# A two-layer decoder trunk on one core: the opening's order, two chunks in a spare buffer, and biases loaded already repeated

## The chip, the core and the metric

The kernel runs on one core of a Trainium2 chip. The metric is the device time of one execution in microseconds (us). A core has a matrix engine (TensorE, PE in the rows; its weight loads are listed apart as PEld), a vector engine (VectorE, DVE), a scalar engine (ScalarE, ACT), GpSimd (POOL) and SyncE (SP), which here only issues transfers. Each engine works through its own instructions in order and waits at an instruction whose operands are not there yet. Transfers run on 16 DMA engines beside them.

## What is computed

```
c_act = silu(c)
for i in range(2):
    sh1, sc1, g1, sh2, sc2, g2 = split(c_act @ ada_w[i] + ada_b[i], 6)
    h = rms_norm(x, norm_mix_g[i]) * (1 + sc1) + sh1
    y = chunk_sgu_mixer(h) if i == 0 else forgetting_attention(h)
    x = x + g1 * y
    h = rms_norm(x, norm_ffn_g[i]) * (1 + sc2) + sh2
    x = x + g2 * ((silu(h @ w_gate[i]) * (h @ w_up[i])) @ w_down[i])
out = rms_norm(x, final_g)

def chunk_sgu_mixer(h):                 # x and h: 256 positions x 2048
    u, v = split(gelu(h @ w_in + b_in)) # w_in 2048 x 4096
    v = layer_norm(v, ln_g, ln_b)
    sv = tril(w_s) @ v + b_s            # in chunks of 128 positions, 16 groups
    return (u * sv) @ w_out
```

Everything is float32. ada_w alone is 2 x 2048 x 12288; a program that reads every weight once moves about 600 MB.

## The kernel before, in words

**Chunks.** Weights come as chunks of 1 MB, a tile of 128 partitions x 4 x 512 named raw, from a pool of five places. SyncE issues their transfers in program order and waits before each until its place is free. An ada chunk (a quarter of one set of four column blocks of a modulation vector) is loaded in ada_chunk (line 153). A weight chunk of w_in is loaded in wchunk (line 303). In the opening the ada chunks are called a0, a1, ... here and the chunks of w_in w0, w1, ..., both in the order of their issue: a0 to a7, w0, a8, w1, a9, a10, w2, a11, w3, a12, a13, w4 and so on.

**What frees a place.** The first 32 ada chunks are multiplied on TensorE (line 169, four matmuls each, into one PSUM bank named misc for a set of four chunks); later ones are multiplied on VectorE (lines 178 and 183). After a set, ada_sum copies the bank by ScalarE into kept (line 195), sums its partitions with four small matmuls (line 198), and VectorE adds the sums to the modulation table mod (line 202). A weight chunk is split: ScalarE casts each half to a rounded high part hi (line 290), and VectorE or GpSimd subtracts to get the low part lo (line 294). Its place is free when both halves are split; there are four buffers each for hi and lo, that is two chunks.

**The first projection.** prepare and modulate make four row blocks of h (tile hA): VectorE scales (line 449), ScalarE adds the shift and writes the high part (line 453), VectorE the low part (line 458). The first such call needs a0 to a3 (shift) and a4 to a7 (scale). v_group multiplies a chunk by hA with three matmuls per row block (lines 351 to 353) into two PSUM banks of the pool mm, which has six; VectorE then adds the result to the tile v (line 547). u_group does the same with lines 335 to 338 and four banks. The loop runs over four quarters of the 2048 rows; in each come four v groups and four u groups, one weight chunk per group, and about one to one and a half ada chunks between two groups. w0 to w3 belong to the first four v groups, v0 to v3, and w4 to w7 to the u groups.

**The opening.** x is loaded into two tiles xt, squared and summed on ScalarE (line 503), and transposed by TensorE into xT (line 519), each bank copied out by ScalarE (line 524). Small tables are transposed on TensorE (lines 122, 126, 138). The bias of v is one row of 2048, loaded to one partition (line 530), repeated to all 128 partitions by four matmuls with ones (line 533), and copied to both halves of v by eight ScalarE copies (line 537). Later the spatial bias b_s (line 575) is repeated in the same way, four times a matmul (line 593) and a ScalarE copy (line 594).

A scheduler orders the instructions of each engine, except inside tc.manual_schedule, where the written order holds; tc.issue_after places an instruction behind another one.

Of the kernel before, what the change touches and what calls it, by code (L numbers as in the profile page):

```python
# [8 lines left out]
F32 = mybir.dt.float32  # L9
# [24 lines left out]
def trunk_kernel(  # L34
# [38 lines left out]
    def misc():  # L73
        return psx.tile([P, 512], F32, tag="misc", name="misc")
# [46 lines left out]
    pt = misc()  # L121
    nc.tensor.transpose(out=pt[:, :96], in_=rows_a, identity=ident[:96, :96])
    nc.vector.tensor_copy(out=cols, in_=pt[:, :96])
    ln_cols = const.tile([P, 32], F32, name="ln_cols")
    pt = misc()
    nc.tensor.transpose(out=pt[:, :32], in_=rows_c, identity=ident[:32, :32])
    nc.vector.tensor_copy(out=ln_cols, in_=pt[:, :32])
# [8 lines left out]
    for i in range(2):  # L136
        pt = misc()
        nc.tensor.transpose(out=pt[:, :96], in_=rows_b[i], identity=ident[:96, :96])
        nc.vector.tensor_copy(out=mod[i], in_=pt[:, :96])
# [9 lines left out]

    def ada_chunk(layer, v, b0, q):  # L150

        raw = rawp.tile([P, 4, 512], F32, tag="raw", name="raw")
# [344 lines left out]
    for q in range(4):  # L497
        ada_next()
    x_ss = const.tile([P, NB], F32, name="x_ss")
    x_rs = const.tile([P, NB], F32, name="x_rs")  # L500
    junk = new_half("junk", F32).rearrange("p a b -> p (a b)")
    for t in range(NB):
        nc.scalar.activation(
            out=junk[:, D * t : D * t + D], in_=xt[t], func=AF.Square,
            accum_out=x_ss[:, t : t + 1],
        )
    rsqrt(x_rs, x_ss, D, NB)
    pt = misc()
    for t in range(NB):
        nc.tensor.matmul(  # L510
            pt[:, P * t : P * t + P], lhsT=x_rs[:, t : t + 1].to_broadcast([P, P]), rhs=ident,
            start=True, stop=True,
        )
    nc.vector.tensor_copy(out=rstd, in_=pt[:, :T])
    for k in range(0, KT, 2):
        pt = misc()
        for b in range(2):
            for t in range(NB):
                nc.tensor.transpose(
                    out=pt[:, T * b + P * t : T * b + P * t + P],  # L520
                    in_=xt[t][:, P * (k + b) : P * (k + b) + P],
                    identity=ident,
                )
        nc.scalar.copy(out=xT[:, k : k + 2, :], in_=pt.rearrange("p (b t) -> p b t", b=2))
# [3 lines left out]
    u = [mgp.tile([P, 8, T], F32, tag="mg", name="u") for _ in range(2)]  # L528
    v = [mgp.tile([P, D], F32, tag="mg", name="v") for _ in range(NB)]
    nc.scalar.dma_start(out=v[1][0:1, :], in_=a_b_in[0:1, D : 2 * D])  # L530
    for a in range(0, D, 512):
        pt = misc()
        nc.tensor.matmul(
            pt, lhsT=ones[0:1, :], rhs=v[1][0:1, a : a + 512], start=True, stop=True
        )
        for t in range(NB):
            nc.scalar.copy(out=v[t][:, a : a + 512], in_=pt)
# [5 lines left out]
    def v_group(cg, k0, nk):  # L543
        ps = proj(mm_b, NB, win_v, D + 512 * cg, hA, k0, k0 + nk, uv_rate(k0, 1.2))
        for t in range(NB):
# [19 lines left out]
    prep(0)  # L565
    for k0, nk in ((0, 4), (4, 4), (8, 4), (12, 4)):
        if k0 == 4:
            pre = new_half("pre", F32).rearrange("p a b -> p (a b)").rearrange(
                "p (a d) -> p a d", a=2
            )  # L570
            nc.sync.dma_start(
                out=pre[:, 0, :].rearrange("t (g s) -> t g s", s=P),
                in_=a_w_s[0].rearrange("g t s -> t g s"),
            )
            nc.sync.dma_start(
                out=pre[0:1, 1, :], in_=a_b_s[0:1].rearrange("o g t -> o (g t)")
            )
# [477 lines left out]
```

## Time and profile before

| what | value |
|---|---|
| runs | 2375.45, 2370.2 and 2375.41 us, median 2375.41 us |
| the profiled execution's own time | 2370.1 us |
| its span, first to last instruction | 2368.4 us |
| TensorE busy | 2293.4 us, 97% of the span |
| VectorE, ScalarE, GpSimd busy | 69%, 47%, 26% |
| mean granted TensorE clock | 0.988 of full speed |
| first matmul of a projection | 47.74 us after the span's start |

The span is what the trace covers; the execution's own time is 1.7 us longer. Busy shares are means over the whole program, and say little of the opening, where the engines fill up one after the other.

### The profile page before, as it was taken

What the parts mean: (1) busy time and instruction counts of PE and PEld (TensorE: products, weight loads), DVE (VectorE), ACT (ScalarE), POOL (GpSimd) and SP (SyncE); (2) the same over time, 40 slices, a digit from 0 to 9 for tenths busy, and PEclk for the clock granted to TensorE, in tenths of its full rate; (3) what the DMA queues carried; (4) which work ended last, traced back from release to release, by engine and by line L of the source; (5) the groups of instructions that cost most, each with busy time, mean ns of one, the idle gap of its engine ahead of it and who ended that gap; (6) DMA issues with size and microseconds to landing.
All of it is one profiled execution on the core that took longest, in us unless ns stands there. A gap on an engine that the chain in (4) does not pass through costs nothing.

```text
span 2368.4 us, 37510 instructions
## 1 busy us (share of the span) xinstructions
PE 2293.4 (97%) x14837; PEld 2035.8 (86%) x14837; DVE 1632.0 (69%) x2382; ACT 1118.5 (47%) x1851; POOL 622.3 (26%) x379
## 2 busy tenths in 40 slices
PE   6999799999999999999999999999999999999998
PEld 3778678999988888888877888899999988888887
DVE  2356986789997777777797776677776844444564
ACT  4433644643554445544454554446444533444443
POOL 1323344444561112122211111220112411212221
PEclk8999899999999999999999999999999999999999
DMA  8878878998878788788787776689765555555552
GB/s 334 304 254 306 293 252 321 338 327 313 314 272 298 269 283 284 270 284 272 274 285 256 249 243 241 217 295 338 257 224 179 195 179 196 178 196 185 189 178 89
DMA packets 305043, 605.69 MB, mean 256 GB/s; under 512 B 11586, under 2 KB 11714, under 8 KB 304610
## 3 DMA queue, kind: packets, MB, share of 16 engines
q1 hardware_dynamic: 304578, 603.13, 73.0%
q8 instruction: 116, 1.90, 0.3%
q14 instruction: 59, 0.48, 0.1%
q0 software_dynamic: 288, 0.16, 0.0%
q10 hardware_dynamic: 2, 0.01, 0.0%
HBM read 601.15 MB, written 2.11 MB: 255 GB/s over the span
## 4 chain that ended last, share of the span: by engine, by line
PE 84%; DVE 9%; DMA 3%; ACT 2%; issue 1%; POOL 0%; SPq 0%; ACTq 0%; DVEq 0%
PE mm L333 31%; PE mm L338 25%; PE mm L336 9%; PE mm L335 9%; PE mm L351 2%; PE mm L352 2%; DVE misc L183 2%; PE mm L353 2%; DVE lo L294 2%; DMA raw<-in_a_w_in_dram 2%; PE misc L169 1%; ACT hi L290 1%; DVE gu L735 1%; DMA raw<-in_a_w_out_dram 1%; DVE m L440 1%
## 5 line engine op out<-in xcount | busy, mean ns | idle before, releaser
L290 ACT CAST hi<-raw 128x1024 fp32r<-128x1024 f32 x752 | 780.2, 1050 | 884.3 <-PE mm L333 493.6
L294 DVE TENSOR_TENSOR lo<-raw,hi 128x1024 fp32r<-128x1024 f32 x566 | 725.3, 1285 | 448.6 <-ACT hi L290 445.1
L338 PE MATMUL mm<-hA,lo 128*128 128x256 f32 x3584 | 983.1, 283 | 0.6 <-DVE lo L294 0.5
L294 POOL TENSOR_TENSOR lo<-raw,hi 128x1024 fp32r<-128x1024 f32 x186 | 471.2, 2534 | 1379.6 <-ACT hi L290 1305.6
L338 PEld LDWEIGHTS mm<-hA,lo 128*128 128x128 f32 x3584 | 681.2, 191 | 11.6 <-issue 1.1
L333 PE MATMUL mm<-hA,hi 128*128 128x512 f32 x1792 | 624.4, 398 | 8.4 <-DVE hA L458 4.5
L335 PE MATMUL mm<-hA,hi 128*128 128x256 f32 x1792 | 502.9, 285 | 7.3 <-DVE gu L735 5.6
L336 PE MATMUL mm<-hA,hi 128*128 128x256 f32 x1792 | 505.7, 284 | 0.5 <-DVE hA L458 0.5
L333 PE MATMUL mm<-m,hi 128*128 128x512 f32 x1248 | 432.7, 396 | 0.0
L333 PEld LDWEIGHTS mm<-hA,hi 128*128 128x128 f32 x1792 | 333.0, 189 | 80.2 <-DVE qk L941 4.6
L338 PE MATMUL mm<-m,lo 128*128 128x256 f32 x1408 | 383.1, 281 | 0.1
L335 PEld LDWEIGHTS mm<-hA,hi 128*128 128x128 f32 x1792 | 341.7, 192 | 16.8 <-DVE gu L735 7.6
L183 DVE SCALAR_TENSOR_TENSOR misc<-raw,cact,misc 128x512 f32<-128x512 f32 x465 | 348.2, 749 | 6.6 <-DMA raw<-in_ada_w_dram 1.0
L336 PEld LDWEIGHTS mm<-hA,hi 128*128 128x128 f32 x1792 | 344.9, 192 | 3.4 <-issue 2.4
L333 PEld LDWEIGHTS mm<-m,hi 128*128 128x128 f32 x1248 | 231.4, 188 | 49.7
L338 PEld LDWEIGHTS mm<-m,lo 128*128 128x128 f32 x1408 | 265.4, 189 | 5.6 <-DVE lo L294 0.3
L735 DVE TENSOR_TENSOR gu<-mm,gu 128x256 f32<-128x256 f32 x288 | 112.7, 415 | 52.4 <-PE mm L338 52.3
L481 DVE SCALAR_TENSOR_TENSOR xT<-mm,mod,xT 128x256 f32<-128x256 f32 x176 | 75.5, 477 | 54.1 <-PE mm L338 54.1
L351 PE MATMUL mm<-hi,hA 128*128 128x512 f32 x256 | 100.9, 401 | 3.1 <-ACT hA L453 3.1
L352 PE MATMUL mm<-lo,hA 128*128 128x512 f32 x256 | 101.6, 398 | 0.0
L353 PE MATMUL mm<-hi,hA 128*128 128x512 f32 x256 | 101.5, 398 | 0.0
L440 DVE TENSOR_TENSOR m<-mf,m 128x256 fp32r<-128x256 f32 x88 | 64.4, 743 | 14.2 <-ACT m L439 13.8
(211 smaller groups left out, 2090.8 us busy)
## 6 DMA issues: line engine op xcount, KB each, us to landing
raw<-in_ada_w_dram SPq DMA_DIRECT2D x192, 1024.0 KB, 6.0
raw<-in_ffn_w_gate_dram SPq DMA_DIRECT2D x88, 1024.0 KB, 5.4
raw<-in_ffn_w_up_dram SPq DMA_DIRECT2D x88, 1024.0 KB, 5.1
raw<-in_ffn_w_down_dram SPq DMA_DIRECT2D x88, 1024.0 KB, 5.0
raw<-in_b_w_in_dram SPq DMA_DIRECT2D x48, 1024.0 KB, 6.0
raw<-in_a_w_in_dram SPq DMA_DIRECT2D x32, 1024.0 KB, 6.9
raw<-in_a_w_out_dram SPq DMA_DIRECT2D x16, 1024.0 KB, 6.9
raw<-in_b_w_out_dram SPq DMA_DIRECT2D x16, 1024.0 KB, 5.7
```

Of the source, the lines that this page charges most:

```text
L183: nc.vector.scalar_tensor_tensor(out=acc, in0=raw[:, k, :], scalar=cact[:, kt : kt + 1], in1=acc, op0=ALU.mult, op1=ALU.add,)
L290: nc.scalar.copy(out=out_hi, in_=src)
L294: ins = eng.tensor_sub(out=out_lo, in0=src, in1=out_hi.bitcast(F32))
L333: nc.tensor.matmul(ps[j], lhsT=hi[:, js], rhs=x, start=start, stop=False)
L335: nc.tensor.matmul(o, lhsT=hi[:, js], rhs=x[:, 0:T], start=start, stop=False)
L336: nc.tensor.matmul(o, lhsT=hi[:, js], rhs=x[:, T:], start=False, stop=False)
L338: nc.tensor.matmul(o, lhsT=lo[:, js], rhs=x[:, 0:T], start=False, stop=(kt == last))
L351: nc.tensor.matmul(ps[t], lhsT=xh, rhs=hi[:, k, :], start=(kt == first), stop=False)
L352: nc.tensor.matmul(ps[t], lhsT=xh, rhs=lo[:, k, :], start=False, stop=False)
L353: nc.tensor.matmul(ps[t], lhsT=xl, rhs=hi[:, k, :], start=False, stop=(kt == last))
L440: nc.vector.tensor_sub(out=dst[:, T:], in0=src, in1=dst[:, 0:T].bitcast(F32))
L735: nc.vector.tensor_add(out=dst, in0=ps[j][:, 0:T], in1=dst)
```

## The change

The opening's TensorE work is written out inside tc.manual_schedule: x is transposed first, in three pieces, with the first ada chunks between them, and the tables follow. xT is copied out of PSUM by VectorE in place of ScalarE, from the banks mm. The first two ada chunks go to a spare tile of hpool (early, in the list places), and raw's five places serve from the third chunk on. The squares of x are written to the tile that later is u.

The bias of v and b_s are loaded by transfers that read the one row once for each of the 128 partitions (partition_broadcast), 1 MB each, on ScalarE's queue, behind the instruction made (the fourth high part of hA). w_s (1 MB) is loaded there too; it was on SyncE's queue. The eight matmuls and the ScalarE copies that repeated the biases are gone. Only v[0] gets the bias; the first v groups add it from there for both halves. The subtractions of the first four half chunks are put on VectorE (hold).

```
+    def table(dst, src):
+        n = src.shape[0]
+        pt = banks(1)[0]
+        nc.tensor.transpose(out=pt[:, :n], in_=src, identity=ident[:n, :n])
+        nc.vector.tensor_copy(out=dst, in_=pt[:, :n])
...
-        raw = rawp.tile([P, 4, 512], F32, tag="raw", name="raw")
+        raw = places.pop(0) if places else rawp.tile([P, 4, 512], F32, tag="raw", name="raw")
...
-    for q in range(4):
-        ada_next()
...
-    junk = new_half("junk", F32).rearrange("p a b -> p (a b)")
+    early = new_half("early", F32)
+    places += [early[:, 0:4, :], early[:, 4:8, :]]
+    u = [mgp.tile([P, 8, T], F32, tag="mg", name="u")]
+    junk = u[0].rearrange("p a b -> p (a b)")
...
-        nc.scalar.copy(out=xT[:, k : k + 2, :], in_=pt.rearrange("p (b t) -> p b t", b=2))
+            nc.vector.tensor_copy(
+                out=xT[:, k : k + 2, :], in_=pt.rearrange("p (b t) -> p b t", b=2)
+            )
...
+    with tc.manual_schedule(engines={nc.tensor.engine}):
+        x_columns(0, 8)
+        ada_next()
+        x_columns(8, 12)
+        ada_next()
+        x_columns(12, 16)
+        table(cols, rows_a)
+        table(ln_cols, rows_c)
+        ada_next()
+        x_scale()
+        for i in range(2):
+            table(mod[i], rows_b[i])
+        for q in range(5):
+            ada_next()
...
-    nc.scalar.dma_start(out=v[1][0:1, :], in_=a_b_in[0:1, D : 2 * D])
-    for a in range(0, D, 512):
-        pt = misc()
-        nc.tensor.matmul(
-            pt, lhsT=ones[0:1, :], rhs=v[1][0:1, a : a + 512], start=True, stop=True
-        )
-        for t in range(NB):
-            nc.scalar.copy(out=v[t][:, a : a + 512], in_=pt)
...
-        for t in range(NB):
-            dst = v[t][:, 512 * cg : 512 * cg + 512]
-            nc.vector.tensor_add(out=dst, in0=ps[t], in1=dst)
+        for t in reversed(range(NB)):
+            s = slice(512 * cg, 512 * cg + 512)
+            dst = v[t][:, s]
+
+            nc.vector.tensor_add(out=dst, in0=ps[t], in1=v[t if k0 else 0][:, s])
...
-    prep(0)
+    made, _ = prep(0)
+    pre = new_half("pre", F32).rearrange("p a b -> p (a b)").rearrange("p (a d) -> p a d", a=2)
+    with tc.issue_after(made.ins):
+        nc.scalar.dma_start(
+            out=v[0], in_=a_b_in[0:1, D : 2 * D].rearrange("o n -> (o n)").partition_broadcast(P)
+        )
+        nc.scalar.dma_start(
+            out=pre[:, 1, :],
+            in_=a_b_s[0:1].rearrange("o g t -> (o g t)").partition_broadcast(P),
+        )
+        nc.scalar.dma_start(
+            out=pre[:, 0, :].rearrange("t (g s) -> t g s", s=P),
+            in_=a_w_s[0].rearrange("g t s -> t g s"),
+        )
+    hold[:] = [((), nc.vector)] * 4
...
-                pt = misc()
-                nc.tensor.matmul(pt, lhsT=ones[0:1, :], rhs=pre[0:1, 1, gs], start=True, stop=True)
-                nc.scalar.copy(out=pre[:, 1, gs], in_=pt)
```

TensorE, from its second instruction to the first matmul of v0, before (L519 are x's transposes, L169 ada chunks of four matmuls each, L533 the bias of v):

```order
L122 MATMUL misc<-ident,rows 128x96
L126 MATMUL misc<-ident,rows 128x32
L138 MATMUL misc<-ident,rows 128x96 x2
L169 MATMUL misc<-raw,cact_142 32x512 x16
L198 MATMUL misc<-ones,kept 128x1 x4
L510 MATMUL misc<-ident,x_rs 128x128 x2
L519 MATMUL misc<-ident,xt 128x128 x32
L533 MATMUL misc<-v,ones 128x512 x4
L169 MATMUL misc<-raw,cact_142 32x512 x16
L198 MATMUL misc<-ones,kept 128x1 x4
L169 MATMUL misc<-raw,cact_142 32x512 x4
L351 MATMUL mm<-hi,hA 128x512
```

The same place of the changed kernel, from the second piece of x on (its lines are one or more higher: L515 for L519, L170 for L169, L199 for L198):

```order
L170 MATMUL misc<-early,cact_131 32x512 x4
L515 MATMUL mm<-ident,xt 128x128 x8
L136 MATMUL mm<-ident,rows 128x96
L136 MATMUL mm<-ident,rows 128x32
L170 MATMUL misc<-raw,cact_131 32x512 x4
L527 MATMUL mm<-ident,x_rs 128x128 x2
L136 MATMUL mm<-ident,rows 128x96 x2
L170 MATMUL misc<-raw,cact_131 32x512 x4
L199 MATMUL misc<-ones,kept 128x1 x4
L170 MATMUL misc<-raw,cact_131 32x512 x16
L199 MATMUL misc<-ones,kept 128x1 x4
L170 MATMUL misc<-raw,cact_131 32x512 x4
```

The bias matmuls are gone, the transposes of x stand ahead of or between the first chunks, and nothing but one short sum stands between the fourth and the fifth ada chunk.

ScalarE in the same stretch, before (L290 are the casts of weight chunks, L195 the copies of ada sums, L537 those of the bias):

```order
L195 COPY kept<-misc 128x512
L524 COPY xT<-misc 128x512 x8
L537 COPY v<-misc 128x512 x2
L290 CAST hi<-raw 128x1024
L537 COPY v<-misc 128x512 x2
L290 CAST hi<-raw 128x1024
L537 COPY v<-misc 128x512 x4
L195 COPY kept<-misc 128x512
L290 CAST hi<-raw 128x1024 x2
L453 ACTIVATE hA<-xr,mod_130 128x256 x4
```

And in the changed kernel:

```order
L196 COPY kept<-misc 128x512
L291 CAST hi<-raw 128x1024 x2
L196 COPY kept<-misc 128x512
L454 ACTIVATE hA<-xr,mod_125 128x256 x2
L291 CAST hi<-raw 128x1024 x2
L454 ACTIVATE hA<-xr,mod_125 128x256 x2
L585 DMA v<-in_a_b_in_dram 128x2048
L588 DMA pre<-in_a_b_s_dram 128x2048
L592 DMA pre<-in_a_w_s_dram 128x16x128
L291 CAST hi<-raw 128x1024 x2
```

The sixteen copies for xT and the bias have left ScalarE; the second copy of an ada sum still stands behind the two casts of w0, and three transfers are issued behind the fourth high part of hA.

## Rows read from the trace of the kernel before

**Rows 1.** The page: the span, and TensorE's busy time over it.

```profile
span 2368.4 us, 37510 instructions
PE 2293.4 (97%) x14837; PEld 2035.8 (86%) x14837; DVE 1632.0 (69%) x2382; ACT 1118.5 (47%) x1851; POOL 622.3 (26%) x379
```

**Rows 2.** Chain of waits, 20 to 60 us: start, duration, what ended last.

```profile
20.83 11.43 DMA raw<-in_a_w_in_dram
...
36.42 1.91 PE misc L169 x8
...
38.34 6.92 DMA raw<-in_a_w_in_dram
...
45.28 1.99 ACT hi L290 x2
...
47.74 0.79 PE mm L351
```

**Rows 3.** Stretches: busy time (and count) of engines, granted clock, DMA share, GB/s.

```profile
10.00:20.00 10.00, 6.35 (x31) 1.80 (x35) 1.34 (x8) 2.90 (x4) 0.00 (x0) 1.00 1.05 408
20.00:30.00 10.00, 8.96 (x56) 5.39 (x48) 0.59 (x2) 5.93 (x11) 0.00 (x0) 1.00 1.05 409
30.05:40.29 10.24, 8.13 (x25) 1.98 (x28) 1.23 (x1) 5.38 (x9) 2.35 (x1) 0.50 0.30 100
40.29:47.10 6.81, 3.68 (x32) 1.37 (x24) 1.95 (x5) 2.40 (x3) 0.00 (x0) 1.00 1.05 404
47.10:53.94 6.84, 6.20 (x18) 3.22 (x19) 4.93 (x7) 2.00 (x5) 2.46 (x1) 0.50 1.05 409
53.94:60.00 6.06, 6.06 (x28) 5.03 (x27) 1.55 (x2) 1.41 (x2) 0.00 (x0) 1.00 1.05 401
117.00:150.00 33.00, 33.00 (x155) 24.06 (x155) 14.26 (x27) 12.80 (x16) 11.04 (x5) 1.00 0.52 185
```

**Rows 4.** Timeline, 0 to 60 us: start, duration, engine, line, and idle time before.

```profile
9.32 1.91 ACT L503 ACTIVATE junk<-xt 128x2048 f32<-128x2048 f32 x1 [1.03 <-DMA xt<-in_x_dram]
...
22.91 5.33 PE L519 MATMUL misc<-ident,xt 128*128 128x128 f32 x32
...
42.00 0.59 ACT L195 COPY kept<-misc 128x512 f32<-128x512 f32 x1 [4.47 <-PE misc L169]
...
42.63 1.05 PE L198 MATMUL misc<-ones,kept 128*128 128x1 f32 x8 [0.71 <-ACT kept L195]
...
43.62 1.06 PE L169 MATMUL misc<-raw,cact 128*32 128x512 f32 x8
...
44.12 0.88 DVE L449 SCALAR_TENSOR_TENSOR xr<-xT,acol,rstd 128x256 f32<-128x256 f32 x2
...
51.45 1.94 PE L169 MATMUL misc<-raw,cact 128*32 128x512 f32 x8
```

**Rows 5.** Timeline, 58 to 71 us, VectorE and GpSimd.

```profile
59.06 1.22 DVE L294 TENSOR_TENSOR lo<-raw,hi 128x1024 fp32r<-128x1024 f32 x1
...
60.77 2.40 POOL L294 TENSOR_TENSOR lo<-raw,hi 128x1024 fp32r<-128x1024 f32 x1 [10.96 <-ACT hi L290]
...
62.98 0.69 DVE L547 TENSOR_TENSOR v<-mm,v 128x512 f32<-128x512 f32 x1 [0.67 <-PE mm L353]
...
63.13 2.00 POOL L579 TENSOR_SCALAR_AFFINE_SELECT pre<-pre 128x2048 f32<-128x2048 f32 x1
...
70.83 0.69 DVE L547 TENSOR_TENSOR v<-mm,v 128x512 f32<-128x512 f32 x1 [0.67 <-PE mm L353]
```

**Rows 6.** Chain of waits, 112 to 160 us: the first of four such rows.

```profile
121.65 1.05 PE misc L593 x2
```

**Rows 7.** TensorE's waits, 222 to 312 us: waiter, releaser, total, times, longest.

```profile
PE misc L214 <- ACT kept L209: 9.7, 1, 9.7
PE mm L641 <- ACT v L628: 4.2, 1, 4.2
```

**Rows 8.** Tile vf: landing of four 0.5 MB transfers, repeated to 128 partitions.

```profile
DMA to landing us min/median/max: 6.3/7.0/7.7
```

More of the change, by code (lines that the diff above doesn't have):

```diff
@@ L120, in trunk_kernel @@
     cols = const.tile([P, 96], F32, name="cols")
-    pt = misc()
-    nc.tensor.transpose(out=pt[:, :96], in_=rows_a, identity=ident[:96, :96])
-    nc.vector.tensor_copy(out=cols, in_=pt[:, :96])
+    cols = const.tile([P, 96], F32, name="cols")
     ln_cols = const.tile([P, 32], F32, name="ln_cols")
-    pt = misc()
-    nc.tensor.transpose(out=pt[:, :32], in_=rows_c, identity=ident[:32, :32])
-    nc.vector.tensor_copy(out=ln_cols, in_=pt[:, :32])
     lng_col, lnb_col = ln_cols[:, 0:16], ln_cols[:, 16:32]
@@ L135, in trunk_kernel @@
     acol = [[const.tile([P, KT], F32, name=f"acol{i}_{j}") for j in range(2)] for i in range(2)]
[L136 to L139, printed above, removed]
+    def table(dst, src):
[3 more added lines that the diff above has]
+        nc.vector.tensor_copy(out=dst, in_=pt[:, :n])
     ada_v = [ada_w[i].rearrange("(kt p) (v n) -> p kt v n", p=P, n=D) for i in range(2)]
@@ L148, in trunk_kernel @@
     lo_last, paced = [], []
+    places = []
     def ada_chunk(layer, v, b0, q):
-        raw = rawp.tile([P, 4, 512], F32, tag="raw", name="raw")
+        raw = places.pop(0) if places else rawp.tile([P, 4, 512], F32, tag="raw", name="raw")
         nc.sync.dma_start(
@@ L494, in new_h @@
         return lambda kt: halves[kt // 8][:, kt % 8, :]
-    for q in range(4):
-        ada_next()
     x_ss = const.tile([P, NB], F32, name="x_ss")
     x_rs = const.tile([P, NB], F32, name="x_rs")
-    junk = new_half("junk", F32).rearrange("p a b -> p (a b)")
+    early = new_half("early", F32)
+    places += [early[:, 0:4, :], early[:, 4:8, :]]
+    u = [mgp.tile([P, 8, T], F32, tag="mg", name="u")]
+    junk = u[0].rearrange("p a b -> p (a b)")
     for t in range(NB):
         nc.scalar.activation(
-            out=junk[:, D * t : D * t + D], in_=xt[t], func=AF.Square,
-            accum_out=x_ss[:, t : t + 1],
+            out=junk, in_=xt[t], func=AF.Square, accum_out=x_ss[:, t : t + 1]
@@ L506, in trunk_kernel, with x_columns @@
         )
     rsqrt(x_rs, x_ss, D, NB)
-    pt = misc()
-    for t in range(NB):
-        nc.tensor.matmul(
-            pt[:, P * t : P * t + P], lhsT=x_rs[:, t : t + 1].to_broadcast([P, P]), rhs=ident,
-            start=True, stop=True,
-        )
[L514 to L517, printed above, removed]
-            for t in range(NB):
[L519 to L523, printed above, removed]
-        nc.scalar.copy(out=xT[:, k : k + 2, :], in_=pt.rearrange("p (b t) -> p b t", b=2))
+    def x_columns(k0, k1):
+        for k in range(k0, k1, 2):
+            pt = banks(1)[0]
+            for b in range(2):
+                for t in range(NB):
+                    nc.tensor.transpose(
+                        out=pt[:, T * b + P * t : T * b + P * t + P],
+                        in_=xt[t][:, P * (k + b) : P * (k + b) + P],
+                        identity=ident,
+                    )
+            nc.vector.tensor_copy(
+                out=xT[:, k : k + 2, :], in_=pt.rearrange("p (b t) -> p b t", b=2)
+            )
@@ new lines, in x_scale @@
+    def x_scale():
+        pt = banks(1)[0]
+        for t in range(NB):
+            nc.tensor.matmul(
+                pt[:, P * t : P * t + P], lhsT=x_rs[:, t : t + 1].to_broadcast([P, P]),
+                rhs=ident, start=True, stop=True,
+            )
+        nc.vector.tensor_copy(out=rstd, in_=pt[:, :T])
+    with tc.manual_schedule(engines={nc.tensor.engine}):
[12 more added lines that the diff above has]
+            ada_next()
@@ L526, in trunk_kernel @@
     win_v = a_w_in[0].rearrange("(kt p) n -> p kt n", p=P)
     hA = new_h("hA")
-    u = [mgp.tile([P, 8, T], F32, tag="mg", name="u") for _ in range(2)]
+    u.append(mgp.tile([P, 8, T], F32, tag="mg", name="u"))
     v = [mgp.tile([P, D], F32, tag="mg", name="v") for _ in range(NB)]
-    nc.scalar.dma_start(out=v[1][0:1, :], in_=a_b_in[0:1, D : 2 * D])
-    for a in range(0, D, 512):
-        pt = misc()
-        nc.tensor.matmul(
-            pt, lhsT=ones[0:1, :], rhs=v[1][0:1, a : a + 512], start=True, stop=True
-        )
-        for t in range(NB):
-            nc.scalar.copy(out=v[t][:, a : a + 512], in_=pt)
@@ L544, in v_group @@
         ps = proj(mm_b, NB, win_v, D + 512 * cg, hA, k0, k0 + nk, uv_rate(k0, 1.2))
-        for t in range(NB):
-            dst = v[t][:, 512 * cg : 512 * cg + 512]
-            nc.vector.tensor_add(out=dst, in0=ps[t], in1=dst)
+        for t in reversed(range(NB)):
+            s = slice(512 * cg, 512 * cg + 512)
+            dst = v[t][:, s]
+            nc.vector.tensor_add(out=dst, in0=ps[t], in1=v[t if k0 else 0][:, s])
             if k0 + nk == KT:
@@ L564, in trunk_kernel @@
     prep = prepare(0, 0, hA)
-    prep(0)
+    made, _ = prep(0)
[7 more added lines that the diff above has]
+            in_=a_b_s[0:1].rearrange("o g t -> (o g t)").partition_broadcast(P),
+        )
+        nc.scalar.dma_start(
+            out=pre[:, 0, :].rearrange("t (g s) -> t g s", s=P),
+            in_=a_w_s[0].rearrange("g t s -> t g s"),
+        )
+    hold[:] = [((), nc.vector)] * 4
     for k0, nk in ((0, 4), (4, 4), (8, 4), (12, 4)):
         if k0 == 4:
[L568 to L577, printed above, removed]
             wst = pre[:, 0, :].rearrange("t (g s) -> t g s", s=P)
```

1 line of the change is left out of this document (removed).

## The prediction

> **What bounds the kernel now.** The page first [rows 1]: TensorE is busy for 2293 of 2368 us, so work taken off TensorE, or time in which it waits, is what can be won. The opening is the largest wait. I read it in the chain of waits between 20 and 60 us [rows 2]: w0 is issued at 20.83 and has landed at 32.26; nothing about it is late. The next link is TensorE at 36.42, which multiplies a4 only then; that frees a place, w1 is issued at 38.34 and lands at 45.26, and two casts, the first high part and 0.5 us later the first projection matmul, at 47.74. The stretches say the same from the transfers' side [rows 3]: the DMA engines are full (share 1.05) from 10 to 30 us and from 40 on, and at 0.30 from 30.05 to 40.29. That is a hole of 0.7 x 10.24 = 7 us. It opens because a4 to a7 lie in their places while TensorE works through what stands ahead of them: x's transposes (5.33 us from 22.91 on [rows 4]), and the bias matmuls L533, whose banks wait for ScalarE copies that stand behind the casts of w0.
>
> From the first matmul on it is TensorE: 6.06 of 6.06 us from 53.94 on, 33.00 of 33.00 from 117 to 150, with the DMA share down to 0.52 there [rows 3]. So an earlier first matmul should move everything behind it, as long as the transfers follow.
>
> **The change, part by part.**
>
> *Where the first matmul moves.* A chunk of 1024 KB takes 1.049 MB / 408 GB/s = 2.57 us of full transfers [rows 3]. Up to w0 the same eleven MB move in the same order through engines that were full already, so w0 lands at 32.3 as before. Counting back from it, a3 landed at 19.4, a4 at 22.0 and a7 at 29.7. In the new order only chunks stand between a3 and a7 on TensorE, and four such matmuls take 1.06 us at the full clock and 1.94 at half [rows 4], both under 2.57, so each is done before the next lands. The transposes lie between the landing of x (9.3 us [rows 4]) and a3: 5.3 us of transposes and four chunks of 1.06 in 10 us. Their copies on VectorE have no row; the nearest is an addition from PSUM of the same shape, 0.69 us [rows 5], so 8 x 0.69 = 5.5 us on an engine with 1.34 busy in that stretch [rows 3]. If that cover failed, they would delay a3, which has 10 us before a7 in hand. I take nothing.
>
> With a4 to a7 freed as they land, a8, w1, a9 and a10 are issued in time and follow w0 without the hole, at 34.8, 37.4, 40.0 and 42.5 (w1 at 45.3 before).
>
> The bound is then w0 itself: on ScalarE the second copy of an ada sum stands behind its two casts. 32.3 + 1.99 (two casts [rows 2]) = 34.25. From here the old offsets hold [rows 4]: the sums follow 0.63 after the copy's start (42.00 to 42.63), the scaling 1.49 later (to 44.12), which makes 36.4; 0.47 for it (half of 0.88, rounded up) and 0.5 for the high part make 37.4. The matmuls of a8, landed at 34.8, stand behind the sums and end between 37.0 and 37.9, by the clock. I take 37.6 for the first matmul: **10.1 us earlier** than 47.74.
>
> *The spatial bias.* Its matmuls L593 go. Each of the four pairs costs 1.05 us on the chain [rows 6], in a stretch where TensorE is full [rows 3]: **4.2 us**. The bias matmuls of v lay before the first matmul and are in the 10.1 already.
>
> *Two more MB of transfers.* The two biases come as 1 MB each where 8 KB came before; w_s moves from one queue to the other. All three are issued behind the fourth high part, about 41 us, into engines that were full there [rows 3]. They add 2 x 2.57 = 5.1 us of transfers before, with w_s, 7.7 us share the engines with w2, a11, w3. What waits is v2. It needs w2 landed, cast and half subtracted: 1.0 + 1.22 [rows 2, 5] = 2.2 us. TensorE wants it when v1 is done, in the old kernel at 62.98 [rows 5], that is 15.2 us after the first matmul, so at 52.8; v3 7.85 us later (70.83 - 62.98), at 60.7. Undisturbed, w2 lands at 45.1 and is ready at 47.3: nothing is lost. If all 7.7 us go first, w2 lands at 52.8 and is ready at 55.0: 2.2 us lost. Then w3, two chunks on, lands at 58.0 and is ready at 60.2, in time. Between 0 and 2.2 I take 0, since nothing in the rows shows one queue shutting out another; 2.2 is kept for the range.
>
> The Trainium skill, page "DMA: Bandwidth & Descriptors", section "Issuing engines are not separate DMA queues", says that transfers started by different engines run on the same 16 DMA engines and interleave. By that rule ScalarE's queue buys no bandwidth, and w2 would pass at about half speed from 41 to 42 us on: it would land near 48 and be ready at 50, also in time. No row here shows two such queues at once.
>
> *Additions that wait for the bias.* v0's and v1's results stay in PSUM until v[0] has landed. Transfers that repeat a row took 6.3 to 7.7 us for 0.5 MB [rows 8], so 1 MB takes 6.3 (the size free) to 15.4 (in proportion): landed between 48 and 57. v0 and v1 hold four of six banks, v2 the other two, so the first to be refused a bank is v3, at 60.7. Nothing lost.
>
> *GpSimd.* w_s must be landed and masked (2.00 us) before GpSimd's part of w3 (2.40) [rows 5]. Landed by 57 at the latest, as the last of the three: both done by 61.4, or by 62.4 if that part waits for the second cast of w3. v3 starts with VectorE's half and asks for GpSimd's 2.7 us later, at 63.4. Nothing lost.
>
> *The clock.* It is at half (1.2 GHz) from 47.10 to 53.94, around the first matmuls, after a stretch with TensorE at 3.68 of 6.81 us [rows 3]. The new opening has TensorE at some 40% of the time between 20 and 37, and I expect about the same stretch at half behind 37.6. Bounds: none, 6.84 / 2 = 3.4 us won; as long as the one of 10.24, 1.7 lost. I take 0.
>
> *Further on.* At 264 us TensorE waits 9.7 and 4.2 us [rows 7]. The scheduler puts that copy kept ahead of casts now, but the second wait ends on the normalised v whatever the first does. VectorE's order there differs by one or two operations of 0.7 us in both directions. 0, with 2 us to either side.
>
> *Sum.* The profiled execution took 2370.1 us (span 2368.4 and 1.7 around it): 2370.1 - 10.1 - 4.2 = 2355.8. The runs stand at two levels, 2370.2 and 2375.4; the profile belongs to the lower, the median to the upper. A new median can fall to either, so I put it between: 2355.8 + 2.6 = **2358.4**.
>
> **Rivals.**
>
> *Less is passed on* (18%). The start moves, but part is lost on the way: the clock stays at half, w2 is late by its 2.2 us, or VectorE, which also bounds the stage behind 264, costs its 2. For it: all three bounds lie there. Against it: each has cover. All three: 2358.4 + 1.7 + 2.2 + 2.0 = 2364.
>
> *The transfers become the bound* (14%). TensorE's earlier start needs w2 to w7 earlier, with 5.1 us more to move. For it: from 53 to 61 us the margin that I found is 0.5 us for w3 when the loads go first. If ScalarE's three loads run as slowly as in [rows 8], 3 MB take up to 46 us, and SyncE's chunks get about half of the engines for that time. A group eats 2.5 chunks, 6.4 us of full transfers, in 7.85 us of TensorE; at half speed 12.8. 46 us at that pace are 3.6 groups with 5 us lost at each, 18 in place of 14.3 won: no change, 2358.4 + 18 = 2376. At half of that duration it is 9 us, 2367. Against it: the share is 0.52 later on.
>
> *Slower: the bias lands too late* (6%). 128 reads of one 8 KB row could be far slower than rows read once. v3 then waits for banks until v[0] is there. It decides at 60.7 + 14.3 = 75 us: a landing behind that makes the kernel slower. At a quarter of the pace of [rows 8], 62 us, v[0] lands at 103, TensorE stands from 60.7, and the time is 2358 + 43 = 2401. Against it: 7.0 us for half a MB, while other chunks were in flight.
>
> **How the numbers follow.** The forecast has the remaining 62%; its own range is 2350.4 (2355.8 less 3.4 for the clock and 2 further on) to 2364 (upper level, with one of the bounds). I give 2350 to 2369, which leaves out the upper half of the transfers' case, the slower one and little below. About 0.3%, 7 us, is what a measurement of this kernel can tell from no change. The forecast and the first rival are faster by more: 80%. The transfers' case centres on no change: 14%. Slower: 6%.
>
> **What would show it.** The first matmul of v0 at 37 to 38 us, with w0 landed at 32.3 and w1 at 37 to 38; a DMA share near 1 from 10 to 55 us without a hole; TensorE full from there on, v1's last addition near 53 and v3 not waiting; the rest of the trace 14 us earlier at the same place. The sum is wrong if TensorE waits between 50 and 75 us for casts of w2 to w4, if the additions of v0 wait for a transfer, or if the wait behind 250 us has grown.

## The result, and the profile after

The changed kernel took 2359.62 us (median of 5 runs, 2355.96 to 2362.97), the kernel before beside it 2373.43 (5 runs): a ratio of 0.9947, 95% interval 0.9936 to 0.9958. It is faster by more than the 0.3% that a measurement here can tell, and 1.2 us above the forecast. The profiled execution took 2359.62 us as well, 10.5 less than that of before.

The page of the changed kernel, to be read against [rows 1]:

```profile
span 2357.9 us, 37458 instructions
PE 2284.9 (97%) x14821; PEld 2036.9 (86%) x14821; DVE 1641.9 (70%) x2392; ACT 1107.0 (47%) x1832; POOL 618.9 (26%) x377
```

TensorE is busy for 8.5 us less, and idle for 2.0 less. The chain of waits from 20 to 72 us (start, duration, what ended last), against [rows 2]:

```profile
20.58 13.08 DMA raw<-in_a_w_in_dram
33.68 1.99 ACT hi L291 x2
35.67 0.49 ACT kept L196
36.20 1.86 PE misc L199 x8
38.07 1.86 PE misc L170 x8
39.93 0.73 PE mm L352
...
62.09 0.80 PE misc L199 x8
...
62.91 0.04 DVE mod L203
...
62.99 0.68 DVE v L564
63.67 2.00 DVE lo L295
...
65.71 0.80 PE mm L353
```

w1 is no longer a link. The start is w0 (landed at 33.66), its casts, the copy kept that stands behind them, the sums and a8. A second chain is new, at v3: the matmul of 65.71 waits for w3's first low part, which on VectorE stands behind the small addition L203 (which waits for TensorE's sums) and an addition of v2.

The stretches (busy time and count of TensorE, its weight loads, VectorE, ScalarE, GpSimd; granted clock, DMA share, GB/s), against [rows 3]:

```profile
20.00:23.60 3.60, 2.56 (x24) 1.13 (x16) 0.16 (x1) 0.59 (x1) 0.00 (x0) 1.00 1.05 410
23.60:30.00 6.40, 3.32 (x16) 0.41 (x16) 0.00 (x0) 0.00 (x0) 0.00 (x0) 0.50 1.05 405
30.00:40.00 10.00, 6.28 (x29) 2.32 (x25) 4.00 (x8) 3.46 (x6) 0.00 (x0) 0.50 1.05 409
40.00:44.10 4.10, 4.10 (x10) 3.24 (x11) 4.10 (x8) 2.62 (x5) 0.00 (x0) 0.50 1.05 409
44.10:50.00 5.90, 5.90 (x30) 3.97 (x30) 0.20 (x1) 0.00 (x0) 0.00 (x0) 1.00 1.03 424
...
64.50:71.40 6.90, 5.69 (x16) 4.00 (x20) 1.15 (x1) 1.99 (x2) 2.44 (x2) 0.51 0.89 337
```

The hole in the transfers is gone (1.05 where 0.30 stood). The clock is at half (1.2 GHz) from 23.6 to 44.1 us, and again from 64.5 to 71.4, behind v3's wait. The timeline of the same stretch, against [rows 4, 5]:

```profile
39.86 0.80 PE L352 MATMUL mm<-hi,hA 128*128 128x512 f32 x1
...
65.71 0.80 PE L353 MATMUL mm<-lo,hA 128*128 128x512 f32 x1 [2.25 <-DVE lo L295]
...
59.66 0.59 ACT L196 COPY kept<-misc 128x512 f32<-128x512 f32 x1 [6.80 <-PE misc L170]
60.14 2.00 ACT L291 CAST hi<-raw 128x1024 fp32r<-128x1024 f32 x2
...
62.22 2.35 POOL L295 TENSOR_TENSOR lo<-raw,hi 128x1024 fp32r<-128x1024 f32 x1 [3.21 <-ACT hi L291]
...
62.99 0.68 DVE L564 TENSOR_TENSOR v<-mm,v 128x512 f32<-128x512 f32 x1
63.59 2.07 DVE L295 TENSOR_TENSOR lo<-raw,hi 128x1024 fp32r<-128x1024 f32 x1
...
76.58 0.68 DVE L564 TENSOR_TENSOR v<-mm,v 128x512 f32<-128x512 f32 x1
...
97.01 0.88 DVE L450 SCALAR_TENSOR_TENSOR xr<-xT,acol,rstd 128x256 f32<-128x256 f32 x2
```

The first projection matmul comes 7.88 us earlier (39.86 for 47.74), v2's last addition 7.84 (62.99 for 70.83), v3's only 2.45 (76.58 for 79.03 in the trace of before). The POOL row is GpSimd's subtraction of w3's second half. VectorE's, which starts beside it at 63.59, takes 2.07 us where the same operation took 1.22 in [rows 5]: 0.85 us of the 2.25 come with that. The last row, the scaling of the second four columns, is a mark for the experiments: it stood at 101.65 before, so 4.64 us are in hand at 100 us.

### The profile page after: what moved, and what is told of

Same layout as the page of the kernel before. It is cut to its first block, busy times and chain, and to the rows that moved or that the text cites. A ratio compares the mean times of both kernels' runs of the same rounds, so it can differ in the third digit from the quotient of the medians.

```text
span 2357.9 us, 37458 instructions
## 1 busy us (share of the span) xinstructions
PE 2284.9 (97%) x14821; PEld 2036.9 (86%) x14821; DVE 1641.9 (70%) x2392; ACT 1107.0 (47%) x1832; POOL 618.9 (26%) x377
## 4 chain that ended last, share of the span: by engine, by line
PE 84%; DVE 9%; DMA 3%; issue 1%; ACT 1%; POOL 0%; SPq 0%; ACTq 0%; DVEq 0%; POOLq 0%
PE mm L334 32%; PE mm L339 25%; PE mm L336 9%; PE mm L337 9%; PE mm L352 2%; PE mm L353 2%; DVE misc L184 2%; PE mm L354 2%; DVE lo L295 2%; DMA raw<-in_ada_w_dram 1%; PE misc L170 1%; DMA raw<-in_a_w_in_dram 1%; DMA raw<-in_a_w_out_dram 1%; ACT hi L291 1%; DVE gu L753 1%
## 5 line engine op out<-in xcount | busy, mean ns | idle before, releaser
L441 DVE TENSOR_TENSOR m<-mf,m 128x256 fp32r<-128x256 f32 x88 | 64.5, 744 | 14.2 <-ACT m L440 13.6
```

## The experiments

Theory R (order): the order by hand closes the hole. Its rival B: the bias matmuls L533 made the hole, and it closes without them whatever the order. For v3: theory O (order on ScalarE and VectorE) against Q (the loads on ScalarE's queue). Ratios are to the runs of before on the same chip; their intervals are 0.1 to 0.2% (2 to 4 us) to either side, so small effects are read from the traces.

### What closed the hole: order_only, loads_only, v_only

order_only keeps the new TensorE order and the two places, with the old biases:

```diff
+    nc.scalar.dma_start(out=v[1][0:1, :], in_=a_b_in[0:1, D : 2 * D])
+    for a in range(0, D, 512):
+        pt = misc()
...
+            nc.scalar.copy(out=v[t][:, a : a + 512], in_=pt)
-    with tc.issue_after(made.ins):
-        nc.scalar.dma_start(
...
+                nc.tensor.matmul(pt, lhsT=ones[0:1, :], rhs=pre[0:1, 1, gs], start=True, stop=True)
+                nc.scalar.copy(out=pre[:, 1, gs], in_=pt)
```

> The changed kernel with its TensorE order and its two spare places, but with the biases as before: a row of 8 KB each, multiplied by ones on TensorE (8 matmuls for v, now behind the sums, 4 for the spatial bias) and copied by ScalarE; w_s on SyncE's queue as before. Theory R (order): the order by hand closes the hole in the transfers from 30 to 40 us; w0 and w1 land as in the changed kernel, the first matmul comes some 2 to 3 us after its 39.86 (bias matmuls of 2.07 a pair stand ahead of it), L593 costs its 4.2 us again, and v3's wait (2.25 and the half clock behind it) is smaller, since nothing shares the engines from 44 to 56: 2359.6 + 4.2 + 2.5 - 3 = 2363, still 7 us or more below before. Rival B (bias matmuls): what the change wins comes from taking the 12 bias matmuls and their 12 copies away; then this kernel is within 4 us of before.

loads_only is the kernel before with the reverse edit: both biases by repeated loads, no bias matmuls, the old order and five places.

> The kernel before with only the loads changed: both biases repeated over the partitions by transfers on ScalarE's queue, no bias matmuls and copies; TensorE's order left to the scheduler, five places. Theory R (order): the 5.33 us of x's transposes still stand between a3 and a4 at 22.9 us, so the places of a4 to a7 come free later, part of the hole stays, and the first matmul is 3 to 5 us later than the 39.86 of the changed kernel: 2363. Rival B (bias matmuls): without L533 TensorE multiplies a4 at 28.2 in place of 36.4, w1 is issued near 29.5, ahead of the end of a8's transfer, so that there is no hole at all; w0 lands at 32.3, the first matmul comes at 38 to 40, and the time is that of the changed kernel, 2358 to 2361.

v_only is the kernel before with the load of v's bias alone:

```diff
-    nc.scalar.dma_start(out=v[1][0:1, :], in_=a_b_in[0:1, D : 2 * D])
-    for a in range(0, D, 512):
...
+    with tc.issue_after(made.ins):
+        nc.scalar.dma_start(
+            out=v[0], in_=a_b_in[0:1, D : 2 * D].rearrange("o n -> (o n)").partition_broadcast(P)
+        )
```

> The kernel before with one thing changed: v's bias comes repeated over the partitions by one transfer on ScalarE's queue behind the high parts of hA, and its 8 bias matmuls and 8 copies are gone. The spatial bias, its matmuls L593, w_s, TensorE's order and the five places stay as they were. Theory H (the hole): these matmuls alone kept a4 to a7 in their places; without them a4 is multiplied at 28.3, w1 is issued near 30, the DMA share stays at 1.05 from 30 to 40 us and the first projection matmul comes near 40 in place of 47.74; at 100 us the kernel is about 6 us ahead of before, and the time 5 us below before (ratio 0.998). Rival S: the win of loads_only is the spatial bias (4.2 us and its copies) and the opening's gain is lost again by 117 us; then this kernel is within 2 us of before.

| kernel | median us (before) | ratio | interval | first matmul | mark at 100 us |
|---|---|---|---|---|---|
| order_only | 2368.26 (2371.01) | 0.9992 | 0.9983 to 1.0001 | 43.14 | 98.06 |
| v_only | 2366.28 (2371.89) | 0.9979 | 0.9969 to 0.9989 | 40.08 | 95.36 |
| loads_only | 2360.89 (2371.01) | 0.9960 | 0.9948 to 0.9972 | 40.14 | 93.95 |
| changed kernel | 2359.62 (2373.43) | 0.9947 | 0.9936 to 0.9958 | 39.86 | 97.01 |

Timeline and stretch of v_only:

```profile
22.77 5.33 PE L519 MATMUL misc<-ident,xt 128*128 128x128 f32 x32
28.04 3.64 PE L169 MATMUL misc<-raw,cact 128*32 128x512 f32 x32
...
40.08 0.80 PE L351 MATMUL mm<-hi,hA 128*128 128x512 f32 x1
...
30.03 0.37 SPq L303 DMA_DIRECT2D raw<-in_a_w_in_dram  x1
```

```profile
30.00:40.00 10.00, 5.26 (x32) 2.24 (x24) 2.65 (x6) 3.23 (x5) 2.44 (x1) 0.76 1.05 407
```

x's transposes still stand between a3 and a4, all 5.33 us of them, and it does not matter: a4 to a7 are multiplied in one piece at 28.04, w1 is issued at 30.03, the share stays at 1.05. With the four bias matmuls (eight rows of the trace, which the expectations count) and their eight copies gone the first matmul comes 7.66 us earlier; the whole change brings 7.88. B holds. The second load adds about what L593 cost: 0.9979 to 0.9960 is 4.5 us, for 4.2 forecast, but the two intervals allow some 1 to 8 us, and loads_only also moves w_s. The traces say the same more closely: the changed kernel's lead over the kernel before, the median over the operations that both have there, grows from 4.9 us at 120 us to 9.5 at 200, by 4.6 across the four pairs of L593.

order_only has no hole from 30 to 40 us either (share 1.05), but the same matmuls now stand ahead of the first projection matmul, at half clock. It has another hole from 50 to 60 us, a share of 0.26, while TensorE is busy throughout:

```profile
37.73 5.48 PE L556 MATMUL misc<-v,ones 1*128 1x512 f32 x6
43.14 0.80 PE L352 MATMUL mm<-hi,hA 128*128 128x512 f32 x1
```

```profile
50.00:60.00 10.00, 10.00 (x48) 5.90 (x50) 3.74 (x5) 1.79 (x2) 4.36 (x2) 1.00 0.26 79
```

It wins 1.9 us, with an interval that includes none; the 2363 of theory R was 5 us too low. So the hole has two cures, and only the one that also takes the matmuls away has a gain here that is clear of the measurement. That the order adds something to the loads is not shown: 0.9947 and 0.9960 overlap.

### The two spare places: five_places

```diff
-    early = new_half("early", F32)
-    places += [early[:, 0:4, :], early[:, 4:8, :]]
```

> The changed kernel without the two spare places: a0 and a1 go into the five places like the rest. Theory: a chunk is issued more than 10 us ahead of its landing either way (w0 would be issued at about 20.6, when a3 has been multiplied, as now), so the transfers stay full to 40 us and the first matmul moves by less than 0.5 us; same time within 2 us. Rival: two places fewer make two chunks fewer in flight; a hole opens between 14 and 20 us or w1 is late, and 2 us or more are lost.

2357.38 us, 0.9952 (0.9935 to 0.9968). w0 is issued at 20.87, the share stays at 1.05 to 40 us: nothing is lost, as the theory has it. The expected move of less than 0.5 us was missed: the first matmul comes at 38.19, since the scheduler put the second copy kept ahead of w0's casts here, by itself; that is the edit of kept_first. So the places are not tested alone against the changed kernel; kept_first, which has that order and the two places, has its first matmul at 38.36 and the same ratio.

### v3's wait: w3_first, late_loads

w3_first puts w3's casts ahead of the third sum's copy, and its low part ahead of v2's additions (the list late holds both until the next weight chunk has been cast):

```diff
+        while late:
+            late.pop(0)()
         return parts
...
+            def third_sum():
+                with tc.issue_after(hi_last[0].ins):
+                    ada_sum(layer, v, b0, acc, banked)
...
+                    if k0 == 0 and cg == 2:
+                        order.enter_context(tc.issue_after(lo_last[-1].ins))
                     nc.vector.tensor_add(out=dst, in0=ps[t], in1=v[t if k0 else 0][:, s])
```

> The changed kernel, with w3's two casts put ahead of the copy kept of the third ada sum on ScalarE, and VectorE's half of w3's low parts ahead of the additions of v2. Theory O (order): the 2.25 us wait of v3 at 63.5 us and the half clock from 64.5 to 71.4 us come from that order alone. Then w3 is cast as it lands, near 58, its first low part is there by 60.5, the wait is gone, the clock stays full from 44 to beyond 75, and v3's last addition comes 5 us earlier, at 71 to 72 in place of 76.58; the time is some 5 us below that of the changed kernel's own runs. Rival Q (queues): w3 lands so late, because the three loads of ScalarE's queue take the engines from 44 to 56 us, that the order does not matter: w3's casts start no earlier than 60 and the wait stays.

late_loads moves two loads behind u0's first copy:

```diff
-        nc.scalar.dma_start(
-            out=pre[:, 1, :],
...
             u_group(cg, k0, nk)
+            if k0 == cg == 0:
+                with tc.issue_after(u_ins[0].ins):
+                    nc.scalar.dma_start(
+                        out=pre[:, 1, :],
...
```

> The changed kernel, with the loads of b_s and w_s issued on ScalarE behind the first bias addition of u0, near 85 us, in place of 42 us; only the 1 MB of v's bias stays at 41 us. Theory Q (queues): w2 lands 2 to 3 us earlier than 50.84 and w3 near 53, and v3's wait of 2.25 us goes, with 5 us of time. Theory O (order): w2 and w3 land that much earlier too, but VectorE still does an addition of v2 ahead of w3's first low part, so that part is done near 64 and 0.5 to 1.5 us of the wait remain. Under both, the loads near 85 us land by 95, ahead of the use at 117, and cost nothing.

The stretch in which the changed kernel lost, in w3_first:

```profile
64.50:71.40 6.90, 6.90 (x40) 3.87 (x39) 2.71 (x4) 2.00 (x2) 2.39 (x1) 1.00 0.91 342
```

No wait and no half clock: the mark stands at 92.37, 4.64 us ahead of 97.01, and w3 is cast as it lands, at 59.08. Theory O holds for the wait. late_loads, timeline:

```profile
48.70 2.00 ACT L291 CAST hi<-raw 128x1024 fp32r<-128x1024 f32 x2 [6.37 <-DMA raw<-in_a_w_in_dram]
...
60.76 0.69 DVE L564 TENSOR_TENSOR v<-mm,v 128x512 f32<-128x512 f32 x1 [6.01 <-PE mm L354]
...
60.84 2.35 POOL L295 TENSOR_TENSOR lo<-raw,hi 128x1024 fp32r<-128x1024 f32 x1 [7.59 <-ACT hi L291]
...
61.37 2.91 DVE L295 TENSOR_TENSOR lo<-raw,hi 128x1024 fp32r<-128x1024 f32 x1
...
96.43 2.31 POOL L594 TENSOR_SCALAR_AFFINE_SELECT pre<-pre 128x2048 f32<-128x2048 f32 x1 [0.63 <-DMA pre<-in_a_w_s_dram]
...
96.79 2.22 DVE L450 SCALAR_TENSOR_TENSOR xr<-xT,acol,rstd 128x256 f32<-128x256 f32 x1
```

w2 lands 2.2 us earlier and w3 5.4 (53.8 for 59.2), yet 2.2 us of v3's wait remain, since the low part still follows an addition: Q falls. But order is not all of it: the low part takes 2.91 us beside GpSimd's (60.84 to 63.19) where 1.22 is usual. By these numbers, an estimate, order alone would leave 0.5 us. That the loads would cost nothing at 85 us was wrong: the mask meets VectorE's scaling (2.22 us where 0.48 is usual), ScalarE's casts stand behind that, and TensorE waits 2.8 us between 84 and 112; another low part costs it 2.6 at 77. 2363.67 us, 0.9967 (0.9954 to 0.998).

w3_first moved two things, ScalarE's copy and VectorE's additions. five_places tells them apart, since there w3 is cast as it lands (59.14):

```profile
59.14 2.00 ACT L291 CAST hi<-raw 128x1024 fp32r<-128x1024 f32 x2 [0.34 <-DMA raw<-in_a_w_in_dram]
...
62.15 2.50 DVE L295 TENSOR_TENSOR lo<-raw,hi 128x1024 fp32r<-128x1024 f32 x1
```

The low part follows the additions all the same, GpSimd's runs from 61.22 to 63.58, and TensorE waits 2.69 us. So VectorE's order, with GpSimd beside it, is enough for the wait; ScalarE's copy is not needed for it.

In time w3_first does not show its 5 us: 2356.68 us, 0.9936 (0.9919 to 0.9953), and its profiled execution is no shorter (span 2358.2). TensorE's waits for low parts between 340 and 410 us, of the changed kernel and of w3_first (waiter, releaser, total, times, longest):

```profile
PE mm L339 <- DVE lo L295: 2.2, 2, 1.3
```

```profile
PE mm L348 <- DVE lo L302: 4.6, 2, 2.8
```

The wait of 2.8 ends at 367.69 and 3.4 us at half clock follow; of the 3.9 us in hand at 350 us 0.5 are left at 390, and 2.6 more are lost between 500 and 650 us, where VectorE is busy for 143 of 150. What in VectorE's order makes these waits was not tried.

### The copy ahead of w0's casts: kept_first

```diff
-    hold[:] = [((), nc.vector)] * 4
+    hold[:] = [((kept_ins[1],), nc.vector)] * 2 + [((made,), nc.vector)] * 2
```

> The changed kernel, with the copy kept of the second ada sum ahead of w0's casts on ScalarE, and w1's casts behind the four high parts of hA. Theory: the first matmul waits for this copy, which stands behind two casts of 1 us that wait for w0 (33.66). a7's matmuls end at 33.04, so the copy ends at 33.6, the sums run from 33.7 to 35.6, a8's matmuls to 37.5, and the first projection matmul comes at 38.2 in place of 39.86: 1.7 us. Rival: the first matmul is bound by w0's casts and low parts on VectorE (34.7 to 37.1) with the scaling behind them, then it comes at 39 or later and at most 0.8 us is won.

```profile
33.16 0.58 ACT L196 COPY kept<-misc 128x512 f32<-128x512 f32 x1 [11.83 <-PE misc L170]
...
38.36 0.79 PE L352 MATMUL mm<-hi,hA 128*128 128x512 f32 x1
...
42.04 2.00 ACT L291 CAST hi<-raw 128x1024 fp32r<-128x1024 f32 x2 [0.92 <-issue]
```

The first matmul is where the theory had it (38.2). But w1's casts, held behind all four high parts, come at 42.04; TensorE waits 0.8 us twice for low parts, and the mark (94.91) gains 2.1. 2361.71 us, 0.9952 (0.9934 to 0.997): not told from the changed kernel.

### The clock: fill

```diff
         for q in range(5):
             ada_next()
+            fill()
+            if q == 4:
+                fill()
+                fill()
...
+    def fill():
+        pt = banks(1)[0]
+        nc.tensor.matmul(pt, lhsT=ident, rhs=xt[0][:, 0:512], start=True, stop=True)
```

> The changed kernel, with one more 128x512 matmul on TensorE behind each of a3 to a6 and three behind a7 (they compute nothing that is used), so that TensorE is busy for most of 20 to 37 us. Theory: the clock fell at 23.6 us because TensorE worked 1.06 of every 2.6 us from there; with the filling it stays at 1.0 to 37 us and beyond, the sums take 1.05 in place of 1.86, a8 1.06 in place of 1.93, the first ten matmuls of v0 0.23 in place of 0.43 each: first matmul 38.1, end of v0 some 3.7 us earlier; w2, ready at 53.2, then takes up to 2 us of it back at v2. Rival: the clock stays at half from 23.6 on, the fillings themselves take 2.1 us each and delay the sums: first matmul at 40 or later.

```profile
23.60:35.90 12.30, 7.58 (x39) 1.52 (x38) 1.40 (x2) 2.47 (x3) 0.00 (x0) 1.00 1.05 407
35.90:42.70 6.80, 6.75 (x14) 3.55 (x14) 5.30 (x10) 2.80 (x4) 0.00 (x0) 0.50 1.05 409
```

Half right: the clock stays at 1.0 to 35.9 us, then falls behind the wait of 4.03 us for the copy kept. The last three fillings stand behind the sums, run at half clock for 5.34 us and put the first matmul at 43.94, 4.1 later than in the changed kernel. And yet the mark (94.60) is 2.4 us earlier: the clock is full from 42.7 on, and in this program VectorE does w3's low part ahead of the additions, so v3 does not wait. 2357.09 us, 0.994 (0.9924 to 0.9956). Four us at the start are worth less than v3's wait.

### The size of the pieces: pieces_2k

```diff
-        nc.scalar.dma_start(
-            out=v[0], in_=a_b_in[0:1, D : 2 * D].rearrange("o n -> (o n)").partition_broadcast(P)
-        )
+        for a in range(0, D, 512):
+            nc.scalar.dma_start(
+                out=v[0][:, a : a + 512],
+                in_=a_b_in[0:1, D + a : D + a + 512].rearrange("o n -> (o n)").partition_broadcast(P),
+            )
...
```

> The changed kernel with each repeated load cut into four of 512 columns, so that its pieces are 2 KB as those of the weight chunks, in place of 8 KB; the bytes are the same. Theory S (size of the pieces decides the shares): from 44 us on the two queues get about half each, some 200 GB/s, where SyncE's queue had 86 to 96 and ScalarE's 328; w2 lands 2 us earlier than 50.84 (near 48.5), v's bias later (near 50), w3 about as before. Rival E (the queue or the engine that issues decides): the shares stay at 328 to 90 and w2 lands at 50 to 51. Theory O has v3's wait unchanged under both, since the order on ScalarE and VectorE is the same.

Queues from 46 to 50 us (packets, MB, share of 16 engines; q1 is SyncE's, q10 ScalarE's), changed kernel and pieces_2k:

```profile
q10 hardware_dynamic: 178, 1.33, 78.4%
q1 hardware_dynamic: 180, 0.37, 23.6%
```

```profile
q1 hardware_dynamic: 428, 0.84, 54.3%
q10 hardware_dynamic: 427, 0.78, 50.9%
```

Theory S holds: the two queues move equally many pieces, so 8 KB pieces get 1.33 MB where 2 KB pieces get 0.37, and half each when the pieces are alike. The edit also makes nine loads of three. w2, issued at 36.86, lands 10.5 us later, near 47.4, 3.4 us ahead of the changed kernel (48.5 was expected), and w3 at 55.2, 3.9 ahead, which was not expected:

```profile
raw<-in_a_w_in_dram SPq DMA_DIRECT2D x1, 1024.0 KB, 10.5
```

The casts do not follow, for a reason nobody expected:

```profile
42.88 10.17 ACTq L591 DMA_DIRECT2D pre<-in_a_b_s_dram  x4
```

ScalarE stands 10 us at issuing four of the loads, and w2's casts, behind them, come at 54.21. 2362.53 us, 0.9966 (0.9954 to 0.9979).

### Versions to beat both: combo, combo_fill, combo_late

combo is w3_first and kept_first together (w1's casts behind two high parts); combo_fill adds one filling behind a4, a5 and a6; combo_late has the two loads behind w4's casts:

```diff
+    hold[:] = [((kept_ins[1],), nc.vector)] * 2 + [((hA_ins[1],), nc.vector)] * 2
...
+            if 1 <= q <= 3:
+                fill()
...
+            if k0 == cg == 0:
+                with tc.issue_after(hi_last[0].ins):
+                    nc.scalar.dma_start(
```

> The changed kernel with both edits of order together: the second copy kept ahead of w0's casts (w1's casts behind the first two high parts), and w3 ahead of the third ada sum and of the additions of v2. Theory: first matmul near 38.2 in place of 39.86, v3's wait gone and no half clock near 65; w2 (ready at 53 at the latest) is still in time for v2, which comes at 53.5. 5 to 6 us ahead of the changed kernel at 100 us; if what was won in w3_first shows again, 1 to 4 us of it are lost between 350 and 550 us to stretches of half clock, and the time is 2 to 5 us below that of the changed kernel (ratio 0.993). Rival: the transfers bind; w2 or w3 is late by what the start gains, and the time is that of w3_first (ratio 0.9936) or no better than the changed kernel.

> The kernel combo with one more 128x512 matmul on TensorE behind each of a4, a5 and a6, which computes nothing that is used. Theory: the clock stays at 1.0 past 23.6 us, and since the sums no longer wait 4 us for a copy it stays so to the first matmul; the sums take 1.05, a8 1.06, the first ten matmuls of v0 0.23 each: first matmul near 37.5 and the end of v0 3 us earlier than in combo. v2 then wants w2 at about 51 and waits 1 to 2 us. At 100 us 1 to 2 us ahead of combo. Rival: the clock falls all the same and the fillings cost 2 us.

> The kernel combo with the loads of b_s and w_s issued behind the casts of w4 on ScalarE, near 68 us, in place of 42 us. Theory: w2 and w3 land 3 us earlier, but nothing waits for them in combo, so TensorE's first 60 us are the same within 0.5 us; the 2 MB come when the engines are nearly free (the share was 0.66 from 70 to 80 us) and land by 78, ahead of the mask and of the use at 117: same time as combo within 1.5 us. Rival: as in late_loads, GpSimd's mask and what stands behind it come late, TensorE waits 2 to 5 us between 90 and 117.

| kernel | median us (before) | ratio | interval | first matmul | mark at 100 us |
|---|---|---|---|---|---|
| combo | 2357.71 (2371.89) | 0.9948 | 0.9936 to 0.9961 | 38.39 | 92.55 |
| combo_fill | 2355.29 (2371.89) | 0.9940 | 0.9928 to 0.9952 | 42.87 | 92.03 |
| combo_late | 2355.65 (2371.89) | 0.9939 | 0.9927 to 0.9951 | 38.12 | 84.40 |

combo wins 4.5 us at the mark, about what was expected, and does not keep it (3.2 us go between 340 and 380). In combo_fill the scheduler put a9's matmuls, which land late, ahead of v0: 42.87 in place of 37.5. combo_late is 12.6 us ahead at its mark, because VectorE's scaling comes earlier there, but TensorE then waits 2.9 us for a cast, before 96 us, and the time is combo's within the measurement. All three lie inside the changed kernel's interval: none is shown to beat it.

## Why the prediction was right, and where not

The time was right (2358.4 for 2359.62); of its terms the first was too large and wrongly put down.

*First matmul, -10.1.* Measured 7.88. Two sizes were off. w0 landed at 33.66, not 32.3: w0's casts start between 33.3 and 34.0 in every kernel here that has chunks queued behind w0, and at 32.3 only in the kernel before, where none is. And the sums and a8 took 1.86 and 1.93, at half clock, for 1.05 and 1.06; 23.6 to 44.1 is a longer stretch at half than the two of before together (20.5 for 17.1 us). The cause was wrong too: the step "In the new order only chunks stand between a3 and a7" takes the order as what closes the hole, and folds the bias matmuls into the same 10.1. v_only has 7.66 of the 7.88 without it.

*L593, -4.2.* Right: 4.6 in the traces between 120 and 200 us, and 4.5 between v_only and loads_only.

*Two MB of transfers, 0.* Right for v2, which did not wait. The Trainium skill, page "DMA: Bandwidth & Descriptors", section "Issuing engines are not separate DMA queues", has the queues interleave on the same engines, and the trace agrees (424 GB/s in all from 44.1 to 50); the half speed that the prediction took from it does not hold for 8 KB pieces against 2 KB, and w2 landed at 50.8, not near 48. The step that failed is "Then w3 ... lands at 58.0 and is ready at 60.2, in time": it landed at about 59, but was ready at 65.7. What was left out is what stands ahead on the engines: an addition on VectorE that waits for TensorE (with a copy on ScalarE ahead of the casts, which five_places shows is not needed for the wait), and GpSimd's subtraction beside VectorE's. Cost: the wait of 2.25 and the half clock behind it, the 5.4 us between v2's lead and v3's.

*Additions that wait for the bias, GpSimd, 264 us: 0.* Right for the bias, which landed 7.2 us after its issue at 41.27, and for the mask, done by 59.0. GpSimd's part of w3 came in time too, but it held VectorE's half by 0.85 us, which the term does not have. The waits at 264 us are 5.7 and 8.4 us for 9.7 and 4.2 in [rows 7], so 14.1 for 13.9.

*The clock, 0.* Off on the slow side: besides the opening's 20.5 us at half for 17.1 there are the 6.8 us behind v3's wait, and a longer stretch near 264 us, where VectorE is busy for most of the time. What that one costs is not shown. Before and changed:

```profile
268.98:282.63 13.65, 3.95 (x17) 3.55 (x18) 11.04 (x20) 8.61 (x21) 2.44 (x1) 0.50 0.95 330
```

```profile
259.11:276.18 17.07, 6.64 (x30) 6.24 (x31) 15.40 (x23) 10.09 (x22) 2.43 (x1) 0.50 0.90 327
```

*The sum.* The profiled execution won 10.5 of 14.3: of the 7.9 us at the first matmul 4.9 are left at 120 us, and L593 adds 4.6. The 2.6 that the prediction added between the profiled execution and the median covered most of the 3.8 missing, by luck. *The rivals.* "Less is passed on" is what the trace shows: in part by the clock, which it names, and mostly by v3's wait, which it does not. The transfers did not become the bound, and the bias was in time.

## What to carry over

A hole in the transfers is closed by whatever lets the places go; look first for work that can leave the engine, then for its order. When a start moves earlier, follow each operand to the instructions that stand ahead of its cast and its subtraction on their engines, and to what GpSimd does beside them, not only to its landing. What is won in an opening can be lost at the next stage that another engine bounds (most of w3_first's 4.6 us were gone at 390 us), so a lead at 100 us is not yet a time.

## What was not expected of the hardware

- Two queues on the same engines shared by pieces here, not by bytes: 178 against 180 pieces, 1.33 MB against 0.37.
- w0 landed 1.1 to 1.7 us later than in the kernel before in all 13 kernels that issue chunks behind it. In the changed kernel the slip begins two chunks earlier: a6 lands at 28.6, for 27.2 before. The cause was not tried.
- VectorE's subtraction of 128x1024 took 1.21 to 1.23 us alone. Where it started while a long operation of GpSimd (subtraction or mask) was under way, it ended 1.08 or 1.09 us after that one's end, in all 29 cases up to 130 us in the 14 traces, and took 1.26 to 3.39 us: as if it had waited for GpSimd to finish.
- In each kernel in which TensorE waited for w3's low part (0.8 to 2.7 us: the changed kernel, late_loads, kept_first, five_places, pieces_2k, loads_only, v_only), the clock stood at half for 3.4 to 6.8 us, beginning within 1.3 us of the end of that wait; in the six others there was neither. A wait alone does not decide it: late_loads waited 2.57 us at 77.13 and pieces_2k 1.73 at 78.33, and the clock stayed full.
